# A bidirectional recurrence by levels: the scores of two levels issued together

## The chip, the cores and the metric

The kernel runs on one core of one Trainium2 chip, in one launch. The metric is the device time in microseconds (us). Before the change it is 1501.87 us, the median of three runs (1501.8 to 1502.08).

A core has a matrix engine (TensorE, in the rows PE for products and PEld for loading the stationary operand), three elementwise engines (VectorE as DVE, ScalarE as ACT, GpSimd as POOL) and SyncE (SP), which here only issues transfers. Each engine works through its own instructions in the order in which they stand; an instruction that waits for a semaphore holds up all that stand behind it on its engine.

## The reference

One layer of a hybrid encoder: 16 learned tokens and 1024 real ones, width 1024. A combined input projection feeds two branches, a neighbourhood attention over a 64-wide grid and a gated linear recurrence in both directions. Their outputs are gated, added, projected, and followed by a squared-ReLU MLP and norms. The change is inside the recurrence, which has 4 heads with keys and values of 128. One chunk of tokens, with `gi` the logarithm of the forget gate:

```python
def step(S, inp):
    qi, ki, vi, gi = inp
    b = jnp.cumsum(gi, axis=-2)
    o_inter = jnp.einsum('bhtk,bhkv->bhtv', qi * jnp.exp(b), S)
    diff = jnp.where(tri[:, :, None], b[..., :, None, :] - b[..., None, :, :], -jnp.inf)
    A = jnp.einsum('bhtk,bhsk,bhtsk->bhts', qi, ki, jnp.exp(diff))
    o_intra = jnp.einsum('bhts,bhsv->bhtv', A, vi)
    b_last = b[..., -1:, :]
    S_new = (jnp.exp(b_last[..., 0, :])[..., None] * S
             + jnp.einsum('bhsk,bhsv->bhkv', ki * jnp.exp(b_last - b), vi))
    return S_new, o_inter + o_intra
```

The kernel's chunks are of 128 tokens. Within a chunk it computes the scores A[s, t] between every key s and query t, each weighted by the product of the gates that lie between them.

## The kernel before

**Projections.** The combined projection runs in blocks of 128 columns (`proj_steps`). A block is eight steps over the 1024 inputs for each piece of up to 512 tokens; a step is three matmuls (lines 122 to 124: high by high, high by low, low by high part of an operand split in two). `proj_steps` is a generator that yields after each step, so other work can be put between steps. The block's weights are split ahead by ScalarE (`hi`, line 112) and VectorE (`lo`, line 113).

**Recurrence by levels.** `hgrn` handles one head in seven levels; I call them the first to the seventh (`lv` 0 to 6), with blocks of h = 1, 2, 4 up to 64 tokens. At a level, the scores between the left and the right neighbour block of h tokens are computed. Keys and queries carry the gate products up to the block's edge: `X` holds the keys on the side that faces the neighbour, `Y` those on the other side, `QQ` the queries of both directions (two tiles, one for each half of the tokens), and `TL` a tree of gate products. From level to level, `keys` makes the next `X` (a copy from `Y`, line 300, and a multiplication, line 301, on VectorE) and the next `Y` (a multiplication on GpSimd, line 303); the queries are multiplied in place (line 432, VectorE, one instruction per half), and each time half of the elements of `QQ` change.

**Scores of a level.** For levels 1 to 6 there are 32 fp32 matmuls, each with 32 stationary columns and 32 moving ones, at four column positions of the array (line 426); each shows as two records, so a level is 64 records. The seventh level has 16 matmuls with 64 columns, 32 records. They write one PSUM bank (`sc`, of three). For levels 1 to 5 a masked copy by VectorE takes the result into `AW` (line 434), and ScalarE copies from there into `A` after the fifth level (line 437); the scores of levels 6 and 7 are copied into `A` by ScalarE alone (line 441).

**What lies between.** After a level's scores come transposes of values, where some are due (`turn_v`, `vpt`), and then projection steps of the same or the next head, as many as `gaps` says: for the first three heads five steps of 512 columns per level mostly, for the fourth head four. Then the keys and the queries of the next level are put out in the program.

**After the levels.** `kmpt` turns the keys of the learned tokens, ScalarE copies it to `kmT` (line 460), the keys are turned (`kpt`, line 472), and the product `pum` (line 464) starts the chain of states `SF` and `SB`. The outputs `po` follow, from `A`, `SF`, `SB` and `QQ`.

**What sets the order.** On TensorE the order of the heads is the order of the program text (`manual_schedule` for that engine). The other engines' instructions are put in order by a scheduler. The four heads follow each other, from about 57 us to 330 us of the span; the attention branch follows.

Of the kernel before, what the change touches and what calls it, by code (L numbers as in the profile page):

```python
# [9 lines left out]
F32 = mybir.dt.float32  # L10
# [3 lines left out]
ALU = mybir.AluOpType  # L14
# [4 lines left out]
P = 128  # L19
# [3 lines left out]
TH = 512  # L23
# [10 lines left out]
NLEV = 7  # L34
# [14 lines left out]
def layer(ctx: ExitStack, tc: tile.TileContext, x, meta, w_in, w_na, w_hg, w_o, w_up, w_dn,  # L49
          g_mix, g_mlp, g_fin, gain, bias, lbl, lmask, wmask, out):  # L50
    nc = tc.nc
    pe, act, dve, pool, sp = nc.tensor, nc.scalar, nc.vector, nc.gpsimd, nc.sync
# [201 lines left out]
    def hgrn(hd, hp, lmask_get, gates, more):  # L254
# [7 lines left out]
        TL = [T0]  # L262
        n = T
# [8 lines left out]
            proj(*last_g.pop())  # L272
            yield

        QQ = [hp.tile([P, 2, TH], F32, tag=f"QQ{hf}", name="QQ") for hf in range(2)]
        qs = [hp.tile([P, TH], F32, tag="q", name="q", bufs=2) for _ in range(2)]

        def ev_q(ps, t0, n):
# [13 lines left out]
        def keys(X, lv, h, n):  # L292


            TT = TL[lv]
            Xn = hp.tile([P, T], F32, tag="X", name="X", bufs=3)
            if lv < NLEV - 1:
                g = n // 4
                mid, mid3, ends = [[4 * h, g], [1, 2 * h]], [[4 * h, g], [h, 2], [1, h]], [[4 * h, g], [3 * h, 2], [1, h]]
                dve.tensor_copy(fap(Xn, h, mid), fap(Y, h, mid))  # L300
                dve.tensor_tensor(fap(Xn, 0, ends), fap(X, 0, ends),
                                   fap(TT, n + 1, [[4, g], [1 - n, 2], [0, h]]), op=ALU.mult)
                pool.tensor_tensor(fap(Y, h, mid3), fap(X, h, mid3),  # L303
                                   fap(TT, 0, [[4, g], [n + 3, 2], [0, h]]), op=ALU.mult)
                return Xn, None
            b = n // 2
            hv = [[2 * h, b], [1, h]]
            KF = hp.tile([P, T], F32, tag="X", name="KF", bufs=3)
            act.copy(fap(KF, h, hv), fap(Y, h, hv))
            dve.tensor_tensor(fap(KF, 0, hv), fap(X, 0, hv), fap(TT, n + 1, [[2, b], [0, h]]), op=ALU.mult)  # L310
            act.copy(fap(Xn, 0, hv), fap(Y, 0, hv))
            pool.tensor_tensor(fap(Xn, h, hv), fap(X, h, hv), fap(TT, 0, [[2, b], [0, h]]), op=ALU.mult)
            return Xn, KF
# [21 lines left out]
        def turn_v():  # L335

            pt, at, copies = None, 4, []
            for vt, c0, n in sorted(ready, key=lambda q: -q[2]):
                if at + max(n, 1) > 4:
                    pt, at = bank("b", "vpt"), 0  # L340
                if n == 0:
                    pe.transpose(pt[:NM, at], vt, ident)
                    copies.append((Vm, pt[:NM, at]))
                for j in range(n):
                    pe.transpose(pt[:, at + j], vt[:, j * P:(j + 1) * P], ident)
                if n:
                    copies.append((V[:, c0:c0 + n], pt[:, at:at + n]))
                at += n
            for dst, src in copies:
                act.copy(dst, src)  # L350
            ready[:], aged[:], turned[:] = aged, turned, []
# [23 lines left out]
        def between(columns):  # L375

            while columns > 0:
                n = next(fill, 0) or next(more, 0)
                columns = columns - n if n else 0
# [30 lines left out]
            gaps = [(KC - 1) * (256 + NM) + TH] + [4 * TH] * 5 + [3 * TH]  # L410
        (aged if first else ready).extend(turned)
        del turned[:]
        for lv in range(NLEV):
            TT = TL[lv]
            m = max(KG, h)
            w = KG if h < KG else h
            sc = score_bank()[:, :8 * w].rearrange("p (g q) -> p g q", q=w)
            for g in range(8):
                for i in range(0, P, m):
                    t0 = g * P + i  # L420
                    qh, q0 = QQ[g // 4], t0 % TH
                    if h < KG:
                        q = fap(qh, q0, [[2 * h, KG // (2 * h)], [TH + h, 2], [1, h]])
                    else:
                        q = qh[:, 0, q0 - h:q0] if i // h % 2 else qh[:, 1, q0 + h:q0 + 2 * h]
                    pe.matmul(sc[i:i + m, g], X[:, t0:t0 + m], q, start=True, stop=True, tile_position=(0, i))
            turn_v()
            between(gaps[lv])
            Xn, KF = pre.pop(0) if pre else keys(X, lv, h, n)
            for hf in range(2):  # L430
                qa = fap(QQ[hf], 0, [[2 * h, n // 4], [TH + h, 2], [1, h]])
                dve.tensor_tensor(qa, qa, fap(TT, hf * n // 2 + 1, [[2, n // 4], [n - 1, 2], [0, h]]), op=ALU.mult)
            if h < KG:
                dve.copy_predicated(AW, lmask_sb[:, lv:lv + 1, :].broadcast_to([P, 8, KG]), sc)
                if 2 * h == KG:
                    for i in range(0, P, KG):
                        act.copy(A[i:i + KG, :, i:i + KG], AW[i:i + KG])
            else:
                for i in range(0, P, h):
                    o = i - h if i // h % 2 else i + h  # L440
                    act.copy(A[i:i + h, :, o:o + h], sc[i:i + h])
            X, h, n = Xn, 2 * h, n // 2
        TC, KB = TL[-1], X
        yield
# [1453 lines left out]
```

## Time and profile before

| what | value |
| --- | --- |
| median of three runs | 1501.87 us |
| the profiled execution | 1503.44 us |
| its span | 1501.6 us |
| busy: PE, DVE, ACT, POOL | 99%, 70%, 45%, 24% of the span |
| granted TensorE clock over the span | 0.999 |
| first and last start of a score matmul of line 426 | 57.9 us, 306.9 us |
| records of line 426 | 1664 |

The profiled execution lies 1.57 us above the median of the runs and 1.84 us above its own span. In a row of the timeline the first two numbers are the start and the duration in us; a matmul's duration includes the way through the array, so matmuls overlap, and what one costs TensorE is the distance from its start to the next start. In a row with square brackets the number there is the engine's idle time before it, and the arrow names what ended it.

### The profile page before, as it was taken

The page shows a single profiled execution, that of the slowest core. Times are in us where ns is not written, and L with a number is a line of the kernel's source. Part 1 is how long each engine was busy: PE and PEld are TensorE (multiplying, and loading weights), DVE is VectorE, ACT ScalarE, POOL GpSimd, SP SyncE. Part 2 cuts the span into 40 slices and gives each one's busy share as a digit, 9 for nine tenths or more (in the row PEclk, how much of TensorE's full clock was granted, in tenths as well). Part 3 has the DMA queues.
Part 4 walks back from the last instruction along what each step waited for, and adds up shares of the span by engine and source line. Part 5 has one row for each costly group of instructions (what it writes and reads, how often), then busy time and mean ns, then how long its engine had stood idle before and what let it go on. Part 6 is the DMA issues. An engine that isn't in the chain of part 4 may idle for free.

```text
span 1501.6 us, 23490 instructions
## 1 busy us (share of the span) xinstructions
PE 1488.3 (99%) x9200; PEld 1249.3 (83%) x9200; DVE 1048.8 (70%) x1612; ACT 669.4 (45%) x1197; POOL 366.3 (24%) x346
## 2 busy tenths in 40 slices
PE   9999999999999999999999999999999999999998
PEld 8888888888888888888888887888888888888886
DVE  7867676756696796675585489777777535877876
ACT  7232313136575576343233355555555534334444
POOL 3313131314413400110000122244444200231134
PEclk9999999999999999999999999999999999999999
DMA  5211111112313237444656124444444667563223
GB/s 171 60 29 58 29 58 29 58 48 101 109 42 96 98 99 252 141 153 154 238 166 213 42 99 168 162 155 154 154 155 155 208 242 247 189 228 114 97 98 141
DMA packets 142591, 195.61 MB, mean 130 GB/s; under 512 B 8192, under 2 KB 90368, under 8 KB 142480
## 3 DMA queue, kind: packets, MB, share of 16 engines
q1 hardware_dynamic: 133216, 172.86, 34.9%
q10 hardware_dynamic: 7088, 13.91, 2.4%
q0 software_dynamic: 2176, 7.34, 1.3%
q8 instruction: 72, 1.18, 0.3%
q14 instruction: 39, 0.32, 0.1%
HBM read 139.56 MB, written 54.53 MB: 129 GB/s over the span
## 4 chain that ended last, share of the span: by engine, by line
PE 89%; DVE 5%; POOL 2%; issue 2%; ACT 1%; DMA 1%; SPq 0%; POOLq 0%; ACTq 0%; DVEq 0%
PE mm L122 10%; PE mm L124 10%; PE mm L123 10%; PE mm L1565 6%; PE pa L1565 6%; PE pc L1565 4%; PE pb L928 4%; PE pb L929 4%; PE pb L1565 4%; PE pb L930 4%; PE pc L929 3%; PE pc L930 3%; PE pc L928 3%; PE pa L929 2%; PE pa L930 2%; PE pa L928 2%
## 5 line engine op out<-in xcount | busy, mean ns | idle before, releaser
L122 PE MATMUL mm<-aT,hi 128*128 128x512 f32 (+2 forms) x600 | 214.6, 358 | 0.0
L124 PE MATMUL mm<-aT,lo 128*128 128x512 f32 (+2 forms) x600 | 211.8, 353 | 0.0
L123 PE MATMUL mm<-aT,hi 128*128 128x512 f32 (+2 forms) x600 | 211.0, 352 | 0.0
L97 DVE TENSOR_TENSOR dl<-ur,dh 128x1024 fp32r<-128x1024 f32 x54 | 69.7, 1290 | 89.6 <-ACT dh L96 89.4
L96 ACT CAST dh<-ur 128x1024 fp32r<-128x1024 f32 x54 | 56.9, 1054 | 165.8 <-issue 91.1
L124 PEld LDWEIGHTS mm<-aT,lo 128*128 128x128 f32 x600 | 113.2, 189 | 12.8
L122 PEld LDWEIGHTS mm<-aT,hi 128*128 128x128 f32 x600 | 113.3, 189 | 12.5
L123 PEld LDWEIGHTS mm<-aT,hi 128*128 128x128 f32 x600 | 113.3, 189 | 11.5
L1354 ACT ACTIVATE uv<-uv 128x512 f32<-128x512 f32 x48 | 30.4, 633 | 79.3 <-DVE uv L1462 52.8
L112 ACT CAST hi<-raw 128x1024 fp32r<-128x1024 f32 x26 | 27.3, 1050 | 64.6 <-PE mm L123 62.2
L1656 POOL TENSOR_TENSOR w<-w,tt 128x512 f32<-128x512 f32 x16 | 23.3, 1459 | 132.7 <-DVE tt L1655 112.0
L854 DVE CUSTOM_DVE_ANT_0 pr<-nsc,NB 128x432 f32<-128x432 f32 (+1 forms) x64 | 35.2, 559 | 28.6 <-issue 28.4
L113 DVE TENSOR_TENSOR lo<-raw,hi 128x1024 fp32r<-128x1024 f32 x26 | 39.8, 1530 | 18.0 <-ACT hi L112 14.0
L303 POOL TENSOR_TENSOR Y<-X,TN 128x512 f32<-128x512 f32 x20 | 31.1, 1557 | 80.3 <-DVE X L300 80.3
L122 PE MATMUL mm<-wh,mT 128*128 128x512 f32 x128 | 50.2, 392 | 0.0
L124 PE MATMUL mm<-o,lo 128*128 128x512 f32 x128 | 50.0, 391 | 0.1
L123 PE MATMUL mm<-wl,mT 128*128 128x512 f32 x128 | 50.1, 391 | 0.0
L124 PE MATMUL mm<-wh,mT 128*128 128x512 f32 x128 | 49.9, 390 | 0.0
L123 PE MATMUL mm<-o,hi 128*128 128x512 f32 x128 | 49.8, 389 | 0.0
L122 PE MATMUL mm<-o,hi 128*128 128x512 f32 x128 | 49.8, 389 | 0.0
L1565 PE MATMUL mm<-dl,dh 128*128 128x512 f32 x124 | 48.4, 390 | 0.0
L1565 PE MATMUL mm<-dh,dl 128*128 128x512 f32 x124 | 48.3, 389 | 0.0
(469 smaller groups left out, 4442.5 us busy)
## 6 DMA issues: line engine op xcount, KB each, us to landing
raw<-in_w_in SPq DMA_DIRECT2D x56, 512.0 KB, 4.0
ur<-usp SPq DMA_DIRECT2D x54, 512.0 KB, 3.6
raw<-in_w_up SPq DMA_DIRECT2D x16, 1024.0 KB, 6.2
usp<-us SPq DMA_DIRECT2D x60, 256.0 KB, 2.4
sg<-gsp SPq DMA_DIRECT2D x16, 512.0 KB, 5.0
w<-in_w_dn SPq DMA_DIRECT2D x16, 512.0 KB, 4.7
usp<-uv SPq DMA_DIRECT2D x30, 256.0 KB, 2.4
gsp<-gv ACTq DMA_DIRECT2D x24, 256.0 KB, 2.4
```

Source lines behind the costliest of these rows:

```text
L96: act.copy(hi, src)
L97: dve.tensor_tensor(lo, src, hi.bitcast(F32), op=ALU.subtract)
L113: dve.tensor_tensor(lo[:, :kc], raw[:, :kc], hi[:, :kc].bitcast(F32), op=ALU.subtract)
L122: pe.matmul(ps, lh, rh, start=first, stop=False)
L123: pe.matmul(ps, lh, rl, start=False, stop=False)
L124: pe.matmul(ps, ll, rh, start=False, stop=last)
L303: pool.tensor_tensor(fap(Y, h, mid3), fap(X, h, mid3), fap(TT, 0, [[4, g], [n + 3, 2], [0, h]]), op=ALU.mult)
L854: dve.tensor_tensor_reduce(out=pr[:, :w], in0=sc[:, :w], in1=NB[:, i, o:o + w], scale=1.0, scalar=3.0e38, op0=ALU.add, op1=ALU.min, accum_ ...
L928: pe.matmul(ps, lhs[0][:, c], rhs[0][:, k], start=first and k == 0, stop=False, skip_group_check=True)
L929: pe.matmul(ps, lhs[0][:, c], rhs[1][:, k], start=False, stop=False, skip_group_check=True)
L930: pe.matmul(ps, lhs[1][:, c], rhs[0][:, k], start=False, stop=k == 3, skip_group_check=True)
L1565: pe.matmul(ps, a[n == 2][:, q, j * P:(j + 1) * P], b[n == 1][:, q], start=first and n == 0, stop=last and n == 2, skip_group_check=True)
```

## The change

The scores of levels 2 and 3 are issued together in front of the third level's projection steps, those of 4 and 5 in front of the fifth's, and those of 6 and 7 in front of the seventh's. The first level keeps its place. At levels 2, 4 and 6 no scores are issued. Since the scores of such a level then still have to read its queries, the queries of the next level go into another pair of tiles (`queries`, two buffers for each half): VectorE multiplies the half that changes from the old into the new tile, and ScalarE copies the half that stays. The masked copies and the copies into `A` are in a function of their own, `take_scores`, which is called for both levels after the joined scores.

```diff
-        QQ = [hp.tile([P, 2, TH], F32, tag=f"QQ{hf}", name="QQ") for hf in range(2)]
+        def queries():
+            return [hp.tile([P, 2, TH], F32, tag=f"QQ{hf}", name="QQ", bufs=2) for hf in range(2)]
+
+        QQ = queries()
...
-        for lv in range(NLEV):
-            TT = TL[lv]
+        def level_scores(lv, X, QQ):
+            h = 1 << lv
...
-            turn_v()
-            between(gaps[lv])
-            Xn, KF = pre.pop(0) if pre else keys(X, lv, h, n)
-            for hf in range(2):
-                qa = fap(QQ[hf], 0, [[2 * h, n // 4], [TH + h, 2], [1, h]])
-                dve.tensor_tensor(qa, qa, fap(TT, hf * n // 2 + 1, [[2, n // 4], [n - 1, 2], [0, h]]), op=ALU.mult)
+            return sc
+
+        def take_scores(lv, sc):
+            h = 1 << lv
             if h < KG:
                 dve.copy_predicated(AW, lmask_sb[:, lv:lv + 1, :].broadcast_to([P, 8, KG]), sc)
...
+        due = []
+        for lv in range(NLEV):
+            TT = TL[lv]
+            due.append((lv, X, QQ))
+            done = []
+            if lv % 2 == 0:
+                done = [(q[0], level_scores(*q)) for q in due]
+                del due[:]
+            turn_v()
+            between(gaps[lv])
+            Xn, KF = pre.pop(0) if pre else keys(X, lv, h, n)
+            Qn = queries() if due else QQ
+            for hf in range(2):
+                at = [[2 * h, n // 4], [TH + h, 2], [1, h]]
+                dve.tensor_tensor(fap(Qn[hf], 0, at), fap(QQ[hf], 0, at),
+                                  fap(TT, hf * n // 2 + 1, [[2, n // 4], [n - 1, 2], [0, h]]), op=ALU.mult)
+                if due:
+                    same = [[2 * h, n // 4], [TH - h, 2], [1, h]]
+                    act.copy(fap(Qn[hf], h, same), fap(QQ[hf], h, same))
+            QQ = Qn
+            for q in done:
+                take_scores(*q)
             X, h, n = Xn, 2 * h, n // 2
```

On TensorE, in the fourth head before, around the scores of the fourth level (`sc`; `vpt` are transposes of values, `mm` the projection):

```order
L122 MATMUL mm<-aT_87,hi 128x512
L123 MATMUL mm<-aT_88,hi 128x512
L124 MATMUL mm<-aT_87,lo 128x512
L426 MATMUL sc<-QQ,X 32x32 x32
L345 MATMUL vpt<-ident,vt 128x128 x2
L342 MATMUL vpt<-ident,vtm 16x128
L122 MATMUL mm<-aT_87,hi 128x512
```

Now there are no scores at this place; the transposes stand directly behind the projection's matmuls:

```order
L122 MATMUL mm<-aT_87,hi 128x512
L123 MATMUL mm<-aT_88,hi 128x512
L124 MATMUL mm<-aT_87,lo 128x512
L348 MATMUL vpt<-ident,vt 128x128 x2
L345 MATMUL vpt<-ident,vtm 16x128
L122 MATMUL mm<-aT_87,hi 128x512
```

Four steps further, where the fifth level's 32 matmuls stood, there are now 64 in a row, those of the fourth level first:

```order
L122 MATMUL mm<-aT_87,hi 128x512
L123 MATMUL mm<-aT_88,hi 128x512
L124 MATMUL mm<-aT_87,lo 128x512
L429 MATMUL sc<-QQ,X 32x32 x64
L122 MATMUL mm<-aT_87,hi 128x512
```

On VectorE, in the fourth head before, from the masked copy of the third level's scores to that of the fourth's (`vt` takes values out of PSUM, `lo` is a split of weights):

```order
L434 COPY_PREDICATED AW<-lmask_sb,sc 128x256
L300 COPY X<-Y 128x16x32
L301 TENSOR_TENSOR X<-X,TN 128x16x2x16
L330 COPY vt<-mm 128x512
L116 SCALAR_TENSOR_TENSOR lo<-raw,hi 128x1024
L432 TENSOR_TENSOR QQ<-QQ,TN 128x32x2x8 x2
L434 COPY_PREDICATED AW<-lmask_sb,sc 128x256
```

Now, from the third level's queries to those of the fifth:

```order
L458 TENSOR_TENSOR QQ<-QQ,TN 128x64x2x4 x2
L435 COPY_PREDICATED AW<-lmask_sb,sc 128x256
L304 TENSOR_TENSOR X<-X,TN 128x32x2x8
L458 TENSOR_TENSOR QQ<-QQ,TN 128x32x2x8
L333 COPY vt<-mm 128x512
L116 SCALAR_TENSOR_TENSOR lo<-raw,hi 128x1024
L458 TENSOR_TENSOR QQ<-QQ,TN 128x32x2x8
L303 COPY X<-Y 128x16x32
L304 TENSOR_TENSOR X<-X,TN 128x16x2x16
L435 COPY_PREDICATED AW<-lmask_sb,sc 128x256
L303 COPY X<-Y 128x8x64
L458 TENSOR_TENSOR QQ<-QQ,TN 128x16x2x16 x2
```

The query multiplication that makes the fifth level's queries (128x32x2x8) is now two instructions with `vt` and `lo` between them, and the key copies (`X<-Y`) of the later levels stand further behind.

On ScalarE, in the fourth head before, from the last keys (`KF`) to `kmT`:

```order
L309 COPY KF<-Y 128x8x64
L437 COPY A<-AW 32x8x32 x3
L366 ACTIVATE gs<-mm 128x512
L437 COPY A<-AW 32x8x32
L441 COPY A<-sc 32x8x32 x2
L350 COPY V<-vpt 128x512
L441 COPY A<-sc 32x8x32 x2
L311 COPY X<-Y 128x8x64
L441 COPY A<-sc 64x8x64 x2
L112 CAST hi<-raw 128x1024
L366 ACTIVATE gs<-mm 128x512
L460 COPY kmT<-kmpt 16x128
```

Now:

```order
L312 COPY KF<-Y 128x8x64
L462 COPY QQ<-QQ 128x8x2x32 x2
L438 COPY A<-AW 32x8x32
L369 ACTIVATE gs<-mm 128x512
L438 COPY A<-AW 32x8x32 x3
L353 COPY V<-vpt 128x512
L314 COPY X<-Y 128x8x64
L442 COPY A<-sc 32x8x32 x4
L442 COPY A<-sc 64x8x64 x2
L112 CAST hi<-raw 128x1024
L369 ACTIVATE gs<-mm 128x512
L484 COPY kmT<-kmpt 16x128
```

Two copies of queries stand ahead of the copies into `A`, and all copies of the sixth level's scores stand behind `X`.

## The prediction

> **What bounds the kernel now.** I read the page's first part and its chain of waits first, to learn which engine sets the end.
>
> ```profile
> PE 1488.3 (99%) x9200; PEld 1249.3 (83%) x9200; DVE 1048.8 (70%) x1612; ACT 669.4 (45%) x1197; POOL 366.3 (24%) x346
> PE 89%; DVE 5%; POOL 2%; issue 2%; ACT 1%; DMA 1%; SPq 0%; POOLq 0%; ACTq 0%; DVEq 0%
> ```
>
> TensorE is busy for 99% of the span and holds 89% of the chain. The other engines matter where they make it wait. So I price the change as TensorE time, and then look for waits. For the price I read TensorE's timeline around one level's scores, in the fourth head (its third level):
>
> ```profile
> 290.13 0.39 PE L123 MATMUL mm<-aT,hi 128*128 128x512 f32 x1
> 290.36 0.39 PE L124 MATMUL mm<-aT,lo 128*128 128x512 f32 x1
> 290.68 0.76 PE L426 MATMUL sc<-QQ,X 128*32 128x32 f32 x64
> 291.37 0.50 PE L122 MATMUL mm<-aT,hi 128*128 128x512 f32 x1
> 291.71 0.40 PE L123 MATMUL mm<-aT,hi 128*128 128x512 f32 x1
> ```
>
> Two wide matmuls stand 0.23 us apart. From the wide matmul at 290.36 to the second one behind the scores, at 291.71, are 1.35 us, of which two wide ones take 0.46. A level's scores therefore cost 0.89 us: 0.69 from their first record to the next wide matmul, 0.09 more on the way in (0.32 instead of 0.23) and 0.11 on the way out (0.34 instead of 0.23).
>
> **What joining saves.** The trace already holds two sets of scores in a row: the undecayed ones of line 399 and the first level's.
>
> ```profile
> 281.43 0.29 PE L124 MATMUL mm<-aT,lo 128*128 128x272 f32 x1
> 281.64 0.73 PE L399 MATMUL sc<-q,kd 128*32 128x32 f32 x62
> 282.23 0.86 PE L426 MATMUL sc<-QQ,X 128*32 128x32 f32 x62
> 283.02 0.44 PE L345 MATMUL vpt<-ident,vt 128*128 128x128 f32 x2
> ```
>
> From the first record to what follows are 1.38 us, 0.69 more than for one set. So the second set of a pair costs 0.69 instead of 0.89, and a join saves 0.20 us: one way in and one way out. Eight joins are of this kind (levels 2 with 3, and 4 with 5, in four heads): 1.6 us.
>
> That a second set is no cheaper than 0.69 can be seen in the same rows: its records need 0.79 (282.23 to 283.02) where the first set's need 0.59. [...] Were the second set as quick as the first, a join would save 0.2 more, and the twelve 2.4 us more; I go by the rows.
>
> The third join of a head puts the sixth level (32 columns) ahead of the seventh (64 columns):
>
> ```profile
> 305.64 0.39 PE L124 MATMUL mm<-aT,lo 128*128 128x512 f32 x1
> 305.96 1.15 PE L426 MATMUL sc<-QQ,X 128*64 128x64 f32 x32
> 307.04 0.50 PE L122 MATMUL mm<-aT,hi 128*128 128x512 f32 x1
> ```
>
> No row shows what going from 32 to 64 columns costs. The bounds are nothing (saving 0.20) and a full way out and in (saving 0). I take the middle, 0.10, since one change of width remains of the two that such a pair has inside: 0.4 us for four heads, bounds 0 and 0.8. [...]
>
> The transposes that stood behind the scores of level 2, 4 or 6 in some heads now stand behind a wide matmul. That costs nothing by these rows, where a transpose starts 0.22 us after a wide matmul:
>
> ```profile
> 308.99 0.39 PE L124 MATMUL mm<-aT,lo 128*128 128x512 f32 x1
> 309.21 0.27 PE L459 MATMUL kmpt<-ident,km 128*16 128x128 f32 x1
> ```
>
> **A wait that goes.** In the fourth head the second level's scores take longer:
>
> ```profile
> 286.72 1.07 PE L426 MATMUL sc<-QQ,X 128*32 128x32 f32 x64
> 287.73 0.51 PE L122 MATMUL mm<-aT,hi 128*128 128x512 f32 x1
> 283.80 3.48 DVE L432 TENSOR_TENSOR QQ<-QQ,T 128x512 f32<-128x512 f32 x2
> ```
>
> They take 1.01 us instead of 0.69, because the queries' second half is ready only at 283.80 + 3.48 = 287.28. Joined, they are issued some 2.7 us later (four steps of three at 0.23), so 0.32 us go. Gross gain: 1.6 + 0.4 + 0.3 = 2.3 us, of which 0.5 us in each of the first three heads and 0.8 us in the fourth.
>
> **What is added.** The multiplications stay the same in number. ScalarE gets two copies of 128x512 in each of three levels and four heads, 24 in all. The nearest row is its copy of `KF`, 128x512 too:
>
> ```profile
> 300.59 0.62 ACT L309 COPY KF<-Y 128x512 f32<-128x512 f32 x1 [4.45 <-POOL Y L303]
> 310.30 0.60 ACT L366 ACTIVATE gs<-mm 128x512 f32<-128x512 f32 x1
> 310.80 0.24 ACT L460 COPY kmT<-kmpt 16x128 f32<-16x128 f32 x1
> ```
>
> It takes 0.62 us; where the next instruction is ready it starts 0.1 earlier (`gs` to `kmT`), so I take 0.55: 13 us on an engine that is 45% busy. They cost something only where TensorE reaches a reader first. The queries of the second level of a joined pair now hang on VectorE (multiplication), then ScalarE (copy).
>
> In the first three heads there are five steps per level, and ScalarE idles long ahead of the instruction that precedes `kmT`:
>
> ```profile
> 93.28 1.05 ACT L112 CAST hi<-raw 128x1024 fp32r<-128x1024 f32 x1 [3.82 <-PE mm L123]
> 168.91 1.05 ACT L112 CAST hi<-raw 128x1024 fp32r<-128x1024 f32 x1 [4.07 <-PE mm L123]
> 244.55 1.05 ACT L112 CAST hi<-raw 128x1024 fp32r<-128x1024 f32 x1 [4.07 <-PE mm L123]
> ```
>
> The late copies of one head (two, 1.1 us, and a later `KF`) fit into 3.8 us. I count no wait there.
>
> The fourth head has four steps per level and no such idle time:
>
> ```profile
> 302.09 1.23 ACT L437 COPY A<-AW 32x256 f32<-32x256 f32 x3 [0.89 <-DVE AW L434]
> ...
> 307.16 1.17 ACT L441 COPY A<-sc 64x512 f32<-64x512 f32 x2
> 309.23 1.05 ACT L112 CAST hi<-raw 128x1024 fp32r<-128x1024 f32 x1 [0.90 <-ACT A L441]
> 311.09 0.48 PE L464 MATMUL pum<-Vm,kmT 16*128 16x128 f32 x2
> ```
>
> `pum` already waits for `kmT` here, as the list of waits says for each head:
>
> ```profile
> PEld pum L464 <- ACT kmT L460: 1.0, 4, 0.2
> ```
>
> Now the same stretch with the change. From the first copy into `A` to the last, ScalarE has 302.09 to 307.16 + 1.17 = 308.33, 6.24 us of work, and `hi`, `gs`, `kmT` take 309.23 to 311.04, 1.81 us. The 0.9 us between are a wait for TensorE, which comes earlier now. So `kmT` ends 8.05 us after the first copy into `A` starts. Two query copies (1.1 us) stand ahead of that, and ahead of these the in-place multiplication of the fifth level's queries, which must wait for the joined scores.
>
> ```profile
> 295.61 1.53 DVE L116 SCALAR_TENSOR_TENSOR lo<-raw,hi 128x1024 fp32r<-128x1024 f32 x1
> 297.06 1.28 DVE L432 TENSOR_TENSOR QQ<-QQ,TN 128x512 f32<-128x512 f32 x2
> 298.25 0.76 PE L426 MATMUL sc<-QQ,X 128*32 128x32 f32 x64
> 299.09 1.47 POOL L303 TENSOR_TENSOR Y<-X,TN 128x512 f32<-128x512 f32 x1 [3.04 <-DVE X L300]
> 299.54 2.17 DVE L432 TENSOR_TENSOR QQ<-QQ,TN 128x512 f32<-128x512 f32 x2
> ```
>
> The fifth level's scores stood at 298.25; with a set and a wait less (-1.21), one set joined (+0.69) and another taken away (-0.89), the pair starts at 296.8. Its queries' second half now stands behind `lo` on VectorE: joined scores of levels 2 and 3 end at 290.9, then a pair of multiplications contended by GpSimd (2.2), a masked copy, keys and the first half (0.3 + 0.6 + 0.6), `vt` and `lo` (0.6 + 1.5) and the second half (0.65) give 297.4, and the copy on ScalarE 298.0. TensorE needs it after three quarters of the pair, at 297.9: a wait of 0 to 0.4 us. The scores end at about 298.5. GpSimd's `Y` for the last keys now follows two key copies on VectorE that stand behind that same second half, and a `Y` of 1.5 between them, so `KF` comes at about 301.5 instead of 300.59; the multiplication runs beside it, 299.9 to 302.1. Then `KF`, two copies and the first `A`: 302.1 + 1.1 = 303.2, 1.1 us later than 302.09. `kmT` ends at 303.2 + 8.05 = 311.2, and `pum` starts at about 311.3 instead of 311.09. TensorE would by itself have been there 0.8 us earlier than before: the fourth head loses all of its 0.8 us and 0.2 more, a price of 1.0 us, bounds 0 and 2.
>
> **Sum.** 2.3 - 1.0 = 1.3 us less. Against the profiled execution's own 1503.44 us, with 1501.6 of span, that is 1502.1 and 1500.3. The median of the runs shown lies 1.57 us below that execution, so 1501.87 - 1.3 = 1500.6 us. Behind the recurrence TensorE goes on without a gap, so that an earlier end is passed on: the attention's bias `NB` is done well before its first reader.
>
> ```profile
> 345.10 3.42 POOL L784 TENSOR_TENSOR NB<-NB,bs 128x384 f32<-128x384 f32 x3
> 355.48 0.46 DVE L854 CUSTOM_DVE_ANT_0 pr<-nsc,NB 128x288 f32<-128x288 f32 x1 [6.83 <-issue]
> ```
>
> **Rivals.**
>
> Nothing is lost (chance 0.22). If the ScalarE chain is shorter than I count, the gross gain stands: 1501.87 - 2.3 = 1499.6, with the free change of width 1499.2. For it: ScalarE's order puts the query copies first. Against it: `kmT` is already awaited.
>
> The queries come late at many joined pairs (0.16), slower than before. The mechanism is VectorE's multiplication beside GpSimd's `Y`: 3.48 or 2.17 us for a pair instead of 1.28. The change puts two pairs of multiplications and two levels of keys between one joined pair and the next. If each runs contended, the second half comes 0.9 to 2.2 us later (2.17 and 3.48 less 1.28). In the fourth head, with nothing to spare, I count 0.9 at each of two pairs beside the 1.0 above; in the other heads, at six pairs, 0.6 each (2.2 less some 1.6 to spare): 2.3 - 1.0 - 1.8 - 3.6 = -4.1, so 1506.0. It decides from 2.3 us of waits in all; half of what it adds gives 1503.3. Against it: the first three heads have a step more per level, and before the change the queries were ready long ahead, here the fifth level's in the second head at 148.5 for 151.15:
>
> ```profile
> 147.22 1.28 DVE L432 TENSOR_TENSOR QQ<-QQ,TN 128x512 f32<-128x512 f32 x2
> 151.15 0.76 PE L426 MATMUL sc<-QQ,X 128*32 128x32 f32 x64
> ```
>
> The change gives nothing (0.07): the joined sets cost 0.89 each, since the ways in and out are there for the records' own loads. 1501.9. The double set at 281.64 speaks against it.
>
> **Chances.** My forecast, fourth head lost and the rest kept, has 0.55: 1500.6, its own range 1499.8 to 1501.6. The range that holds eight of ten reaches to the first rival's lower end and into the slow one: 1499.2 to 1503.0. A measurement of this kernel tells about 0.2% from no change, 3.0 us. Faster than 1498.9 needs the first rival with something more: 0.03. Slower than 1504.9 needs most of the second: 0.06. Within: 0.91.
>
> **What would show it.** In the changed profile: no wide matmul between the two sets of a pair, a joined pair of 1.4 us from its first record to the next wide matmul; `pum` in the fourth head starting at the same distance from that head's first scores as before (29.4 us), where the first three heads are each 0.5 us shorter; waits of TensorE for a query copy only in the fourth head. I am wrong if such waits stand in the first three heads, if the seventh level's scores start over 0.3 us late behind the sixth's, or if `pum` comes 0.8 us earlier.

## The result, and the profile after

The changed kernel takes 1499.66 us, the median of 22 runs (1498.99 to 1500.69), beside 1501.97 us for the kernel before (22 runs, 1501.27 to 1504.8). The ratio is 0.9983, with a 95% interval from 0.9977 to 0.9989: 2.6 us less, from 1.7 to 3.5 (the two medians lie 2.3 us apart). So the kernel is a little faster, but by less than the 0.2% (3.0 us) below which the prediction calls it no change. The time lies within the predicted range of 1499.2 to 1503.0 us, 0.9 us below the predicted 1500.6 us and 0.1 us below the forecast's own narrower range, which began at 1499.8. The profiled execution took 1499.23 us, with a span of 1497.5 us.

The page's first part and its chain of waits, after the change:

```profile
PE 1485.7 (99%) x9200; PEld 1249.4 (83%) x9200; DVE 1047.2 (70%) x1612; ACT 682.2 (46%) x1221; POOL 366.8 (24%) x346
...
PE 92%; DVE 4%; ACT 2%; issue 1%; POOL 1%; POOLq 0%; ACTq 0%; DVEq 0%
```

TensorE has the same 9200 matmuls and is busy 2.6 us less. ScalarE has 24 instructions and 12.8 us more: the copies of the queries, 0.53 us each.

Where the time went is seen by cutting TensorE's work at fixed matmuls: the first record of a head's undecayed scores (line 399 before, 402 now), `pum` of the fourth head, the last transpose of the recurrence's output (`opt`), and the last product of the attention (`pov`). Lengths in us, worked out from the records; the second column is another profile of the kernel before, from the experiments below:

```
                              before  before again  after
start to first head             57.3      57.2      57.3
first head                      73.06     73.06     72.38
second head                     75.63     75.59     74.87
third head                      75.63     75.67     74.85
fourth head, up to pum          29.44     29.31     28.80
from pum to the last opt        21.0      21.0      21.0
attention, to its last product 232.6     231.5     231.3
the rest                       937.0     936.8     937.0
```

The four heads give 0.68, 0.72 to 0.76, 0.78 to 0.82 and 0.51 to 0.64 us: 2.7 to 2.9 us. The attention's 1.3 us against the first profile is not the change's: the second profile of the kernel before has most of them too.

A joined pair in the timeline of TensorE, fourth head, levels 2 and 3:

```profile
286.85 0.39 PE L124 MATMUL mm<-aT,lo 128*128 128x512 f32 x1
287.17 1.36 PE L429 MATMUL sc<-QQ,X 128*32 128x32 f32 x128
288.46 0.50 PE L122 MATMUL mm<-aT,hi 128*128 128x512 f32 x1
288.80 0.40 PE L123 MATMUL mm<-aT,hi 128*128 128x512 f32 x1
```

From its first record to the next wide matmul are 1.29 us, where a set alone has 0.69: the second set costs 0.60, and joining saves 0.29, not 0.20. By the records the two sets last 0.57 and 0.56 us from the first record to the last, with 0.04 between them. A set alone has the same 0.57, followed by 0.13 before the next wide matmul. That tail is now paid once for two sets, beside the 0.09 in and the 0.11 out.

The third join, levels 6 and 7, same head:

```profile
301.76 0.39 PE L124 MATMUL mm<-aT,lo 128*128 128x512 f32 x1
302.08 1.84 PE L429 MATMUL sc<-QQ,X 128*32 128x32 f32 x96
303.85 0.50 PE L122 MATMUL mm<-aT,hi 128*128 128x512 f32 x1
304.19 0.40 PE L123 MATMUL mm<-aT,hi 128*128 128x512 f32 x1
```

The row has the sixth level's 64 records and the seventh's 32 under one form. Together they take 1.77 us to the next wide matmul, 1.98 with the way in and out, against 0.89 and 1.28 for the two alone: 0.19 to 0.20 saved. Between the 32-column and the 64-column records are 0.13 us, where two sets of one width have 0.04: by this difference the change of width costs some 0.08.

The end of the fourth head, ScalarE and TensorE:

```profile
298.70 0.62 ACT L312 COPY KF<-Y 128x512 f32<-128x512 f32 x1 [3.23 <-POOL Y L306]
299.23 1.14 ACT L462 COPY QQ<-QQ 128x512 f32<-128x512 f32 x2
300.27 0.40 ACT L438 COPY A<-AW 32x256 f32<-32x256 f32 x1
...
303.58 2.69 ACT L442 COPY A<-sc 32x256 f32<-32x256 f32 x6
306.29 1.05 ACT L112 CAST hi<-raw 128x1024 fp32r<-128x1024 f32 x1
307.37 0.60 ACT L369 ACTIVATE gs<-mm 128x512 f32<-128x512 f32 x1
307.86 0.24 ACT L484 COPY kmT<-kmpt 16x128 f32<-16x128 f32 x1
...
307.55 0.33 PE L496 MATMUL kpt<-ident,X 128*128 128x128 f32 x1
308.15 0.48 PE L488 MATMUL pum<-Vm,kmT 16*128 16x128 f32 x2 [0.28 <-ACT kmT L484]
```

From `KF` on ScalarE has no idle time in front of any instruction until `kmT`, 9.4 us later, and TensorE waits 0.28 us for it. That is the price of the added copies, but a smaller one than predicted.

### The profile page after: what moved, and what is told of

Read it like the earlier page. It is cut to its first block, busy times and chain, and to the rows that moved or that the text cites. A ratio compares the mean times of both kernels' runs of the same rounds, so it can differ in the third digit from the quotient of the medians.

```text
span 1497.5 us, 23520 instructions
## 1 busy us (share of the span) xinstructions
PE 1485.7 (99%) x9200; PEld 1249.4 (83%) x9200; DVE 1047.2 (70%) x1612; ACT 682.2 (46%) x1221; POOL 366.8 (24%) x346
## 4 chain that ended last, share of the span: by engine, by line
PE 92%; DVE 4%; ACT 2%; issue 1%; POOL 1%; POOLq 0%; ACTq 0%; DVEq 0%
PE mm L122 11%; PE mm L124 11%; PE mm L123 10%; PE mm L1589 6%; PE pa L1589 6%; PE pc L1589 4%; PE pb L952 4%; PE pb L953 4%; PE pb L1589 4%; PE pb L954 4%; PE pc L952 3%; PE pc L954 3%; PE pc L953 3%; PE pa L952 2%; PE pa L954 2%; PE pa L953 2%
```

## Experiments

Except where times of several runs are given, an experiment is one profiled execution, and the lengths of the heads are worked out as in the table above.

**Is it the joining?** Every level's scores at their own place again; the copies and the extra tiles stay.

```diff
-            if lv % 2 == 0:
+            if True:
                 done = [(q[0], level_scores(*q)) for q in due]
...
-            Qn = queries() if due else QQ
+            apart = lv % 2 == 1
+            Qn = queries() if apart else QQ
...
-                if due:
+                if apart:
```

> Every level's scores stand at their own place, as before the change, but the queries of levels 2, 4 and 6 go into other tiles, with ScalarE's copies. Read by distances on TensorE: from the first record of line 402's scores in one head to that in the next (before 73.07, 75.63, 75.63 us; with the change 72.38, 74.87, 74.85), and in the fourth head from there to pum (29.45; 28.80). Theory J, the gain is the joining itself (0.29 us per pair of 32 columns, 0.20 per third pair): the first three distances stay within 0.1 us of before, the fourth is 29.4 to 29.9, because the copies delay kmT and the wait at the second level goes only in part. Theory W, the gain comes from queries that need not wait for TensorE to read the old ones: the three distances are 0.4 us or more shorter than before.

It takes 1502.4 us. The heads last 73.06, 75.53, 75.60 and 29.37 us, as before the change. So the gain is from the joining, not from the extra tiles or their places, and the copies on their own cost nothing that shows. The second level in the fourth head:

```profile
286.63 1.07 PE L429 MATMUL sc<-QQ,X 128*32 128x32 f32 x64
287.63 0.50 PE L122 MATMUL mm<-aT,hi 128*128 128x512 f32 x1
```

It is 1.00 us again, with the wait of 0.34 us inside, which the joined pair does not have.

**Why did the double set of the kernel before show 0.69 for its second half?** One projection step is moved between the undecayed scores and the first level's, so that each stands alone.

```diff
+        gaps[0] -= TH if first else 256 + NM
+        between(1)
         (aged if first else ready).extend(turned)
```

> One projection step of three matmuls is moved from behind the first level's scores to between line 402's scores and the first level's. In the changed kernel's profile the first level's 64 records take 0.67 us behind other scores, the sets of levels 2 to 5 only 0.57 in either place of a pair. [...] Theory P, the first level's own pattern (its moving columns change direction at every element) is slow wherever it stands: 0.65 to 0.68. In both a way in and out is paid again: the first three distances grow by 0.2 to 0.35 us over the changed kernel's, the total by about 1 us.

```profile
280.73 0.76 PE L402 MATMUL sc<-q,kd 128*32 128x32 f32 x64
...
281.65 0.29 PE L123 MATMUL mm<-aT,hi 128*128 128x272 f32 x1
281.78 0.28 PE L124 MATMUL mm<-aT,lo 128*128 128x272 f32 x1
282.00 0.89 PE L431 MATMUL sc<-QQ,X 128*32 128x32 f32 x64
282.81 0.44 PE L348 MATMUL vpt<-ident,vt 128*128 128x128 f32 x2
```

This kernel takes 1500.81 us. The first level's set alone takes 0.81 us to the next instruction; every other set of its size that stands alone and waits for nothing takes 0.69. It is slow in both places: behind the undecayed scores the rows of before give it 0.79. (Its queries alternate between the two directions from column to column; whether that is why was not tried.) Theory P holds. The first three heads became 0.27, 0.30 and 0.30 us longer, the same 0.29 for a join taken away. In the fourth head a wait of 0.39 us appeared in the next pair as well, 0.56 in all.

**How much room do the copies have?** Each copy is made twice.

```diff
                     act.copy(fap(Qn[hf], h, same), fap(QQ[hf], h, same))
+                    act.copy(fap(Qn[hf], h, same), fap(QQ[hf], h, same))
```

> The changed kernel with each of ScalarE's 24 query copies made twice: 0.5 to 0.6 us more per copy. Theory A, ScalarE's copies delay kmT in the fourth head and nothing else: the three first distances stay within 0.1 us of 72.38, 74.87, 74.85, the fourth grows from 28.80 by 0.8 to 1.3 us (two copies of the sixth level). Theory N, kmT is late for another reason (the last Y of GpSimd): the fourth distance grows by less than 0.3. If the copies also bind in the first three heads, their distances grow by 0.5 or more each.

1517.04 us, 15 us more than before the change and 17 more than with it. The first three heads, where both theories saw room, lost 5.4, 5.1 and 6.4 us, the fourth 1.0. The first head's third join, ScalarE's timeline and then TensorE's:

```profile
82.31 0.62 ACT L312 COPY KF<-Y 128x512 f32<-128x512 f32 x1 [6.12 <-POOL Y L306]
...
84.67 1.05 ACT L112 CAST hi<-raw 128x1024 fp32r<-128x1024 f32 x1
85.62 0.59 ACT L222 ACTIVATE sf<-mm 128x512 f32<-128x512 f32 x1
86.11 0.59 ACT L223 ACTIVATE sn<-mm 128x512 f32<-128x512 f32 x1
86.72 0.81 ACT L438 COPY A<-AW 32x256 f32<-32x256 f32 x2
87.56 0.62 ACT L463 COPY QQ<-QQ 128x512 f32<-128x512 f32 x1
88.09 0.61 ACT L462 COPY QQ<-QQ 128x512 f32<-128x512 f32 x1
88.73 0.62 ACT L463 COPY QQ<-QQ 128x512 f32<-128x512 f32 x1
...
88.23 0.69 PE L429 MATMUL sc<-QQ,X 128*64 128x64 f32 x16 [3.06 <-ACT QQ L463]
89.40 0.69 PE L429 MATMUL sc<-QQ,X 128*64 128x64 f32 x16 [0.48 <-ACT QQ L463]
```

The copies do not follow each other: between the first ones and the last three stand the cast of the next weights, two evictions of projection work and copies into `A`. In the changed kernel itself the second copy stands at the same place, and TensorE needs it soon after:

```profile
79.45 0.62 ACT L312 COPY KF<-Y 128x512 f32<-128x512 f32 x1 [4.50 <-POOL Y L306]
...
82.77 0.59 ACT L222 ACTIVATE sf<-mm 128x512 f32<-128x512 f32 x1
83.26 0.59 ACT L223 ACTIVATE sn<-mm 128x512 f32<-128x512 f32 x1
83.88 0.81 ACT L438 COPY A<-AW 32x256 f32<-32x256 f32 x2
84.71 0.62 ACT L462 COPY QQ<-QQ 128x512 f32<-128x512 f32 x1
...
84.48 1.84 PE L429 MATMUL sc<-QQ,X 128*32 128x32 f32 x96
```

It ends at 85.33, and by the records the first matmul that reads it starts at 85.69: 0.36 us to spare. In the first head the change was nearer to a loss than either the prediction or the expectation knew; in the second and third head 2.3 us are left at this place.

The loss with the doubled copies is not their own length alone. `KF`, which stands ahead of them on ScalarE, starts 2.8 to 2.9 us later in each of these three heads, measured from the head's start, because GpSimd's `Y` ends later: in the first head two small GpSimd operations ahead of it took 1.6 and 2.5 us instead of 0.2 and 0.5, and in the second and third head `Y` itself took 3.4 instead of 1.5. Why they did is open. And behind these waits, 3.2 to 3.5 us of TensorE within one group of scores, the granted clock is 0.5 for 3.4 us, in the third head for 6.8 us (over the whole span 0.995, in the change 0.999), with wide matmuls 0.43 us apart instead of 0.23: I estimate from these distances 1.7 us of the loss in each of the first two heads and 2.5 in the third.

**What holds `pum` in the fourth head?** First, its two last copies go to GpSimd.

```diff
-                    act.copy(fap(Qn[hf], h, same), fap(QQ[hf], h, same))
+                    copy = pool.tensor_copy if hd == NHG - 1 and lv == 5 else act.copy
+                    copy(fap(Qn[hf], h, same), fap(QQ[hf], h, same))
```

> The changed kernel with the fourth head's two copies of the sixth level's queries on GpSimd, which has no work between its last Y (ends at 298.7 us in the changed profile) and its X (starts at 302.98). Theory A (ScalarE's two copies make kmT late): kmT comes up to 1.1 us earlier, the wait of pum falls to 0.2 us as before the change, and the fourth distance is 28.2 to 28.5 instead of 28.80. Theory N (it is late for another reason): 28.7 to 28.9. A GpSimd copy that takes over 2 us each would be late for the seventh level's scores: then the distance grows.

1500.18 us; the first three heads as in the change, the fourth 28.64 us, between the two theories. ScalarE, rid of 1.14 us, gave only 0.16:

```profile
299.83 1.23 ACT L438 COPY A<-AW 32x256 f32<-32x256 f32 x3 [0.29 <-DVE AW L435]
...
303.09 0.62 ACT L314 COPY X<-Y 128x512 f32<-128x512 f32 x1 [0.36 <-PE sc L429]
303.61 2.69 ACT L442 COPY A<-sc 32x256 f32<-32x256 f32 x6
...
307.90 0.24 ACT L485 COPY kmT<-kmpt 16x128 f32<-16x128 f32 x1
```

It now waits for VectorE's masked copy and for the scores of the third join, whose six copies into `A` then come together. So the second suspect is that join itself. In the fourth head alone, levels 6 and 7 are taken apart, with the copies kept:

```diff
-            if lv % 2 == 0:
+            last = hd == NHG - 1 and lv == 5
+            if lv % 2 == 0 or last:
...
-            Qn = queries() if due else QQ
+            Qn = queries() if due or last else QQ
...
-                if due:
+                if due or last:
```

> In the fourth head alone the sixth and seventh level are taken apart again, while ScalarE keeps its two copies of the queries at the sixth level. The first three heads as in the changed kernel (72.4, 74.9, 74.9). Theory S: what holds the mean's product there is that a joined pair hands all six copies of its scores to ScalarE at once, behind the seventh level's scores; with the sixth level's four taken earlier the wait of 0.28 us goes, and the head lasts 28.8 + 0.2 (the join lost) - 0.25 = 28.7 to 28.8 us. Theory C: it is the two copies of the queries; then the wait stays as it is and the head lasts 29.0 us.

1499.89 us; the fourth head has 28.90 us, between the theories again. The wait at `pum` went from 0.28 to 0.18 only:

```profile
298.65 0.62 ACT L312 COPY KF<-Y 128x512 f32<-128x512 f32 x1 [3.23 <-POOL Y L306]
...
302.38 0.74 ACT L442 COPY A<-sc 32x256 f32<-32x256 f32 x2
...
307.90 0.24 ACT L485 COPY kmT<-kmpt 16x128 f32<-16x128 f32 x1
...
308.19 0.48 PE L489 MATMUL pum<-Vm,kmT 16*128 16x128 f32 x2 [0.18 <-ACT kmT L485]
```

Four of the copies into `A` are made earlier, and `kmT` still ends 9.49 us after `KF` starts (9.40 in the change). ScalarE is simply full from `KF` to `kmT`: neither what stands in its queue first nor last matters much, only that `KF` comes when GpSimd's `Y` is there, and that 9.4 us of work follow. By the rows of `pool_copies`, with 1.14 us of it taken away the joined scores are the next bound. Neither theory alone is right; each names one of two bounds that lie some 0.2 us apart.

**A second profile of the kernel before.** The same kernel, for the attention's 1.3 us and for the heads.

> The kernel before once more, unchanged, for a second profile. Theory Z: the 1.3 us by which the attention stretch (from the last transpose of the recurrence's output to the last product of the attention) was shorter in the changed kernel than in the first profile of the kernel before is chance of that profile: this profile shows the stretch near the 231.2 to 231.8 us of the four experiments, not 232.58, and the four heads as before (73.06, 75.6, 75.6 and 29.4 us). Rival theory T: the change shortened that stretch as well; then it lies near 232.6 us again.

1501.95 us, heads and attention as in the table's second column. Theory Z holds.

**The third join alone.**

```diff
-            if lv % 2 == 0:
+            if lv != 5:
```

> Only the sixth and seventh level are joined (scores of the second to fifth level each at their own place, with copies only at the sixth). Theory A, what the profile of the changed kernel gives (a change of width costs no more than a change of set): each of the first three heads is 0.20 us shorter than before, 72.85, 75.4 and 75.4 us. Theory B, the prediction's (0.10 for it): 72.95, 75.5 and 75.5. The fourth head: 29.2 to 29.6 us, since its wait at the second level (0.34 us) is back, and the ScalarE work behind the join still holds the mean's product.

1502.89 us. The first three heads have 72.82, 75.30 and 75.30 us: 0.24, 0.29 to 0.33 and 0.33 to 0.37 less than before. That is A's 0.20 and a little more, not B's 0.10. In the second and third head the seventh level's set took 1.33 us before, not 1.28, which is 0.05 of the rest. The fourth head has 29.35 us, as before: there the join is not worth anything by itself. The time as a whole is no shorter, since in this one execution the attention and the rest lay 0.6 and 1.2 us above the second profile of the kernel before.

**One join more.** In the first three heads the scores of levels 2, 3 and 4 are issued together, and those of 5, 6 and 7. The queries need a third pair of tiles; to make room for it an unused pad of 56 words, on the other side of the memory, was made 8 words.

```diff
-    padp.tile([P, 56], F32, name="pad")
+    padp.tile([P, 8], F32, name="pad")
...
-            return [hp.tile([P, 2, TH], F32, tag=f"QQ{hf}", name="QQ", bufs=2) for hf in range(2)]
+            return [hp.tile([P, 2, TH], F32, tag=f"QQ{hf}", name="QQ", bufs=3) for hf in range(2)]
...
-            if lv % 2 == 0:
+            if lv % (3 if hd < NHG - 1 else 2) == 0:
```

> In heads one to three the second, third and fourth level's scores are issued together, and the fifth, sixth and seventh's (two groups where the change has three; the queries get three buffers); the fourth head as in the change. Theory E (each set that joins a group saves what the way in and out cost, 0.29 us, and the queries are in time): one join more in each head, 0.29 shorter each, 72.1, 74.6 and 74.6 us, 0.9 us less in all, about 1498.8 us. Theory Q (the queries of the last level of a group pass three multiplications and three rounds of copies, and ScalarE's second copies stand behind the cast and the evictions of projection work): the last group of a head waits for its queries by 1 us or more, and the kernel is slower than the changed one, 1502 us or more.

1505.07 us (10 runs, 1502.64 to 1507.09), a ratio of 1.0017 with an interval from 1.0007 to 1.0026. The second and third head have 74.50 us each, 0.37 and 0.35 less than in the change, somewhat more than Theory E's 0.29. The first head has 74.44, 2.06 more: behind its first group TensorE stands still.

```profile
70.70 1.97 PE L429 MATMUL sc<-QQ,X 128*32 128x32 f32 x192
...
74.97 0.50 PE L122 MATMUL mm<-aT,hi 128*128 128x512 f32 x1 [2.30 <-issue]
```

It is a projection's matmul that waits, not a query's reader, and the row names nothing that ended the wait; VectorE, whose semaphore its record names, had given its last signal 1.5 us earlier. So this is not Theory Q, and its cause stays open. And a loss was not foreseen at all: from the last product of the attention to the end it takes 941.9 us instead of 937.0, far from anything that was edited. Two more kernels take this apart.

**Three together in the middle heads, with the memory as in the change.**

```diff
-            return [hp.tile([P, 2, TH], F32, tag=f"QQ{hf}", name="QQ", bufs=2) for hf in range(2)]
+            return [hp.tile([P, 2, TH], F32, tag=f"QQ{hf}", name="QQ", bufs=3) for hf in range(2)]
...
-            if lv % 2 == 0:
+            if lv % (3 if 0 < hd < NHG - 1 else 2) == 0:
...
-        SB = hp.tile([P, 8, P], F32, tag="SB", name="SB")
+        SB = hp.tile([P, 7, P], F32, tag="SB", name="SB")
```

> Three levels' scores together, as before, but only in the second and third head (there the queries were in time), and with the memory layout of the change kept: SB, of whose eight blocks one is never used, is made one block smaller, so that the third buffer of the queries fits without a smaller pad. Theory E: these two heads are 0.3 us shorter than in the change (74.5 and 74.5 against 74.87 and 74.85), the first and last as in the change, what comes behind as in the change; 0.6 to 0.7 us less in all. Theory M, the rival on the 4.9 us behind the heads in three_together: these come from the heads' third buffer (from what lies where within the heads' pool); then the stretch from the last product of the attention to the end is 941 to 942 us again instead of 937.

**The change with the small pad and nothing else.**

```diff
-    padp.tile([P, 56], F32, name="pad")
+    padp.tile([P, 8], F32, name="pad")
```

> The change with nothing but the unused pad of 56 words made 8 words, as in three_together: tiles on the right-hand side of the memory lie 192 bytes further. Theory R: that is where the 4.9 us behind the heads in three_together came from (433 wide matmuls in the 100 us from 600 on where the change has 441, at a granted clock of 1.00 in both); then this kernel lies 4 to 6 us above the change, about 1504 us, with 941 to 942 us from the last product of the attention to the end, and the four heads as in the change. Theory M: nothing happens, 1499.7 us and 937 us.

**The change once more beside them.**

> The changed kernel once more, beside the other two. Theory: 72.4, 74.9, 74.9 and 28.8 us again for the heads, 1499.7 us.

The change took 1499.52 us (11 runs, 1498.51 to 1500.25; ratio to before 0.9979, interval 0.997 to 0.9988), with heads of 72.36, 74.83, 74.86 and 28.81 us.

`three_in_middle` took 1499.01 us (11 runs, 1497.88 to 1499.82; ratio 0.9976, interval 0.9967 to 0.9985). Its heads have 72.33, 74.49, 74.50 and 28.81 us, 0.34 and 0.36 less in the middle ones, and 937.6 us for the rest. A group of three sets in its second head:

```profile
143.89 1.89 PE L429 MATMUL sc<-QQ,X 128*32 128x32 f32 x192
145.71 0.44 PE L348 MATMUL vpt<-ident,vt 128*128 128x128 f32 x2
```

It takes 1.82 us, where two sets took 1.29. The third set is not cheaper than the second, though: by the records only 0.01 and 0.02 us lie between these three sets, where the pairs have 0.04, so each of the two added sets costs 0.56 to 0.57. So such a group has two joins worth 0.32 to 0.33 each where the change has one worth 0.29, which makes the 0.36 a head. In the first head of `three_together`, the same three levels have 0.04 between the sets, and each added set costs 0.60. Inside the pairs and inside that group the trace has an instruction in TensorE's queue that only waits for a semaphore, in this group none; whether that is the cause was not tried. This is the fastest kernel of the study; the 0.5 us to the change are near what the heads show (0.7), but the runs of the two overlap.

`small_pad` took 1503.08 us (10 runs, nine of them from 1502.55 to 1504.26 and one of 3011.64, whose cause is not known), 3.6 us more than the change beside it, with the heads as in the change and 940.3 us for the rest. So most of what `three_together` lost behind the heads is the pad's: 3.3 of 4.9 us, by the stretches behind the attention (940.3 and 941.9 against 937.0). Theory R holds, a little below its 4 to 6 us; Theory M falls, since the third buffer with the old pad gives 937.6. The last 1.6 us stay open. The view of stretches from 600 to 700 us (duration; busy time of PE and number of its matmuls; granted clock; share of the DMA engines; GB/s), in the change and then with the small pad:

```profile
600.00:700.00 100.00, 99.89 (x441) 1.00 0.43 138
```

```profile
600.00:700.00 100.00, 99.98 (x433) 1.00 0.42 134
```

One group of matmuls of that stretch (busy us, mean ns of one), in the change and with the small pad:

```profile
L952 PE MATMUL pb<-at,hi 128*128 128x512 f32 x60 | 23.3, 389 | 0.0
```

```profile
L952 PE MATMUL pb<-at,hi 128*128 128x512 f32 x60 | 23.6, 394 | 0.0
```

TensorE is busy all the time at the same clock, but does 433 matmuls where it did 441. By the records, the 288 wide matmuls of `pb<-at` and `pc<-at` start 233 ns apart instead of 227, 3% more, and those with `wb` 229; the other large groups of 128x512 products change by less than 2 ns. The first give some 1.9 us, the second some 1.3: together they are the stretch's 3.3 us. The shift by 192 bytes is all that was edited.

## Why the prediction was right or wrong

- **The time and the class.** 1499.66 us lies in the range, and "within 0.2%" came true. The predicted sum was 1.3 us; the heads give 2.7 to 2.9. Two terms were wrong, the price of a second set and that of the fourth head's ScalarE chain, and both in the same direction; the range was wide enough to hold it, the forecast's own one (1499.8 to 1501.6) was not.
- **"A join saves 0.20 us."** Wrong: 0.29 each. The failed step is the one that took the 0.69 of the second set of lines 399 and 426 for the price of a second set. It was the price of the first level's set, which takes 0.81 where others take 0.69 even when it stands alone. The rows that I quoted could not tell position from kind, since the same level always stood second. The joined groups, rows of 128 and 192 records, kept their pace to the end: 0.55 to 0.57 us from the first record of a set to its last. The case that I set aside, a second set as quick as the first, is what happened; it saved 0.09 more for each join, where I had put 0.2 for it.
- **"A change of width: 0.10 saved, bounds 0 and 0.20."** The saving was 0.20, the number of the upper bound, but not for the reason of that bound, a free change of width. Of the 0.29 that a join of one width saves, the change of width takes 0.08 to 0.09, close to the 0.10 that I put for it; the term was too small because it started from 0.20 instead of 0.29. What TensorE does in the added gap of 0.08 us, no run shows.
- **The wait in the fourth head's second level goes.** Right: the pair there is 1.29 us, and with the scores apart the 0.34 us are back.
- **Transposes behind wide matmuls cost nothing.** Nothing showed.
- **"The fourth head loses all of its 0.8 us and 0.2 more."** Wrong by size. The mechanism was right: ScalarE fills up, `kmT` is late, `pum` waits; the queries' second half behind `lo` leaves a gap of 0.14 us in the pair of levels 4 and 5, which makes it 0.11 longer, within the 0 to 0.4. But with the joins as measured (two of 0.29, one of 0.20, the wait of 0.34: 1.12 us in all), the head gained 0.51 to 0.64, so the price was 0.5 to 0.6 instead of 1.0. Three stages of the forecast came early, seen from the time of the head's start before: `KF` by 0.5 us (301.0 for 301.5), the first copy into `A` by 0.65 (302.55 for 303.2), `kmT` by 0.8 (its end at 310.4 for 311.2). `lo` took 1.21 us instead of the 1.53 that I took from before, and the multiplications ran beside `KF`'s chain earlier than I had put them.
- **No wait in the first three heads.** Right for the query copies, for a reason that is not the one given. (The first head's second pair has 0.14 us between its two sets instead of 0.04, in both profiles of the change; its last query copy had ended 1.4 us before, and what held it is open.) The idle time ahead of `hi` that I named as cover comes later in the queue. What counts is where the second copy of a pair stands, behind `KF`, a cast and two evictions, and there 0.36 us were left in the first head. I had worked out the copies' price where the cover is there, and not what it costs if the cover is gone: with the copies doubled, and `KF` late besides, it was 5 to 6 us in each of these heads.
- **The rivals.** The 1499.6 and 1499.2 of "nothing is lost" are near the result, but by two errors that cancel: some was lost (0.5 to 0.6 us), and the joins gave more. "Queries come late" did not happen, though the margin against it was thinner than my text has it. "Gives nothing" is ruled out by the kernel with the copies alone.
- **The signs named beforehand.** A pair of 1.4 us: 1.29. `pum` at 29.4 us from the head's start: 28.8, so the sign "0.8 earlier" came nearly true. First three heads 0.5 us shorter: 0.7 to 0.8. The seventh level's scores started 0.13 us behind the sixth's, not 0.3. No wait for a query copy in the first three heads.

## What to carry to other kernels

Here each group of small column-tiled matmuls between wide ones paid about 0.3 us beside its own records (0.09 on the way in, 0.13 in the tail, 0.11 on the way out), and each set of the same width that joined a group, of up to 192 records, saved 0.29 to 0.33 us; so gathering them helped as long as their operands were in time. Before a property is read from a row where two things coincide (second in place, and another pattern), find the same pattern alone. And the room of an added instruction is not the idle time of its engine (ScalarE was busy 46% of the span), but the distance from the end of what stands ahead of it in that queue to its first reader, here 0.36 us beyond the copy itself in the first head; that distance was gone when something ahead of it, here `KF`, came 2.8 to 2.9 us late.

## What was not expected of the hardware

- The placement of tiles in memory alone changed matmuls: 192 bytes of shift, the same instructions, a granted clock of 1.00 in both, and 233 or 229 instead of 227 ns from one 128x512 matmul to the next for some operands; 3.6 us in the whole kernel. Which access meets which was not tried.
- Sets of equal matmuls (32 of fp32, 32 by 32 columns) were not equally quick: 0.81 us for the first level's set even alone, 0.69 for all others that stand alone and wait for nothing. What in the operands makes the difference was not tried.
- A set that follows another cost 0.60 us in the pairs and 0.56 to 0.57 in the groups of levels 2 to 4 in the second and third head, with 0.69 for one alone.
- The same GpSimd operations differed severalfold between two kernels: two small ones of the first head took 0.2 and 0.5 us in the change and 1.6 and 2.5 us with the copies doubled, the last `Y` of the second head 1.5 and 3.4 us. Behind TensorE's waits of 3.2 to 3.5 us in that second kernel the granted clock was 0.5 for 3.4 us or more.
